# Seven block products for pairs of token blocks in the gate, and sums on GpSimd instead of VectorE, in a fp32 transformer layer

## The chip, the cores and the metric

The kernel runs on one core of one Trainium2 chip. The metric is the device time of one execution in microseconds (us), the median of several runs. The engines of a core are called by the profile's names: PE (TensorE, the matrix multiplier), DVE (VectorE), ACT (ScalarE), POOL (GpSimd) and SP (SyncE, which here issues most DMAs). Each engine works through its own list of instructions in order; an instruction that waits holds up all that stand behind it on its engine.

## What is computed

One layer of a transformer with 1024 tokens, a model width of 1024 and a feed-forward width of 4096, in fp32:

```
h = LN(alpha*x + concat(pool, attention) @ w_out)
h = LN(alpha*h + square(relu(h @ w_ff1)) @ w_ff2)
h = h + sigmoid(h @ w_ple_gate + b) * (p @ w_ple)
```

The change touches the end of the second line and the third line. There, `w_ple_gate` is 1024 x 1024, `p` is 1024 x 256 and `w_ple` is 256 x 1024.

## The kernel before

**Products.** Each fp32 product is made of three matmuls with shortened operands: an operand is split into a high part (a cast on ACT, `high`, line 98) and a low part (a subtraction of the high part from the operand, `low`, line 103, nearly always on the DVE). `mm3` (lines 112 to 115) then issues high x high, high x low and low x high. `add` (line 118) is any sum or difference of two tiles on the DVE. In the profile a group is named by its line, so all low parts made on the DVE have line 103 and are told apart by the tile that they write: `x` is the low part of a feed-forward weight (tile "x7"), `w` that of activations, `c` that of a gate weight, `ws` that of gate activations.

**Last feed-forward product.** The two feed-forward products are already made of block products of the kind that needs seven in place of eight, with sums of operands. The second one runs over units u = 0 to 55, seven products (their order is `SEQUENCE`, the last is product 2) by eight slices of the width 4096. A unit is 24 matmuls of 128x512. While TensorE works on unit u, `prepare(u + 1)` (line 781) makes the next operands: the sum of two activation blocks into a staging tile `st` of 128x1024 (line 118, two such tiles in turn), its high and low part, and the high and low part of the weight, which a DMA brought three units ahead. Units 48 to 55 are product 2. Beside them run: the second layer norm of token blocks 0 to 3 (`norm2`, `layer_norm`, lines 400 to 420), which lie in the tile `pre`; its last two steps are a scalar-tensor-tensor with the scale (line 419) and an add of the shift (line 420, shown as line 118), both on the whole 128x1024 block; the transposes of token blocks (`flip`, line 424, and a round trip through device memory); and the loads and splits of the gate's weights (`gate_load`, two more low parts `c` of 128x1024 for each call).

**Gate stage.** It goes through the token blocks n = 0 to 7 one after the other. Each block has two column halves of 512; a half takes 8 blocks of the inner dimension x 3 matmuls for the gate and 2 x 3 for `p @ w_ple`, so 60 matmuls of 128x512 for a token block (in the last block the second half is made in two pieces of 256 columns). `result` then adds the bias (line 929), takes the sigmoid on ACT (930), multiplies (931), adds the residual (932) and stores. The layer norm of blocks 4 to 7, the transposes and the splits of the next block run beside it.

**What sets the order.** The code is written as one stream; a scheduler with its own model of times places each engine's instructions, so the order on an engine is not that of the code. The layer norm's power (line 412) is POOL's only operation in this part of the program; POOL's earlier work consists of the pooling sums (line 361), a few splits, and DMA issues.

Of the kernel before, what the change touches and what calls it, by code (L numbers as in the profile page):

```python
# [7 lines left out]
F32 = mybir.dt.float32  # L8
F32R = mybir.dt.float32r
# [3 lines left out]
P = 128  # L13
# [46 lines left out]
}  # L60
BLOCK = {"a11": 0, "a12": 1, "a21": 2, "a22": 3}
NPRE = 8
NLAST = NPAIR - 4
AHEAD = 4

# [2 lines left out]
def layer(ctx, tc, xT, x, pT, w_in, w_pool, pscale, sinks, w_out, ln1, w1, w2, ln2, w_ple, w_gate, bgate, bias, rcount, out):  # L68
# [11 lines left out]
    def big(shape, dt=F32R):  # L80
        return sb.tile(shape, dt, tag="c", bufs=6, name=nm("c"))
# [14 lines left out]
    def high(dst, src, scale=None):  # L96
        if scale is None:
            nc.scalar.copy(out=dst, in_=src)  # L98
        else:
            nc.scalar.mul(out=dst, in_=src, mul=scale)  # L100

    def low(eng, dst, src, hi):
        return eng.tensor_tensor(out=dst, in0=src, in1=hi.bitcast(F32), op=ALU.subtract)  # L103

    def load_split(dst_h, dst_l, src, shape, eng, st=None, queue=None):
        st = stage(shape) if st is None else st
        load = (queue or nc.sync).dma_start(out=st, in_=src)
        high(dst_h, st)
        low(eng, dst_l, st, dst_h)
        return load  # L110

    def mm3(o, ah, al, bh, bl, first, last, more=False):
        nc.tensor.matmul(o, ah, bh, start=first, stop=False, skip_group_check=more)  # L113
        nc.tensor.matmul(o, ah, bl, start=False, stop=False, skip_group_check=more)  # L114
        nc.tensor.matmul(o, al, bh, start=False, stop=last, skip_group_check=more)  # L115

    def add(o, a, b, op=ALU.add):
        nc.vector.tensor_tensor(out=o, in0=a, in1=b, op=op)  # L118
# [278 lines left out]

    hn = [None] * NT

    def layer_norm(y, gb, root=False):  # L400
        st = small([P, 2, 6])
        for i in range(2):
            nc.vector.bn_stats(out=st[:, i, :], in_=y[:, i * HALF : (i + 1) * HALF])
        mv = small([P, 8])
        nc.vector.bn_aggr(out=mv[:, 0:2], in_=st.rearrange("p a b -> p (a b)"))
        v, r0, e, r, m = (mv[:, i : i + 1] for i in range(2, 7))
        nc.vector.tensor_scalar(out=v, in0=mv[:, 1:2], scalar1=LN_EPS, scalar2=None, op0=ALU.add)
        if root:
            nc.vector.reciprocal(out=r0, in_=v)
            nc.scalar.activation(out=r0, in_=r0, func=AF.Sqrt)  # L410
        else:
            nc.gpsimd.tensor_tensor(out=r0, in0=v, in1=mhalf, op=ALU.pow)
# [4 lines left out]
        nc.vector.tensor_scalar(out=m, in0=mv[:, 0:1], scalar1=-1.0, scalar2=None, op0=ALU.mult)  # L417
        nc.scalar.activation(out=y, in_=y, func=AF.Identity, bias=m, scale=1.0)
        nc.vector.scalar_tensor_tensor(out=y, in0=y, scalar=r, in1=gb[0], op0=ALU.mult, op1=ALU.mult)
# [98 lines left out]
    def temp(shape=(P, HALF)):  # L518
        return p1.tile(list(shape), F32, tag="t", bufs=6, name=nm("t"))
# [121 lines left out]
    def bank(shape=(P, HALF)):  # L641
        return pf.tile(list(shape), F32, tag="f", bufs=8, name=nm("f"))
# [81 lines left out]
    def incoming(shape=(P, 2, HALF)):  # L724
        return part(shape, F32)
# [44 lines left out]
    def hid(q, t, k):  # L770
        return hidden[q][:, k, t] if q in hidden else FF[q, k, t]
# [49 lines left out]
    def gate_load(j):  # L821
        if j == 0:
            gates["b"] = nat([P, D])
            nc.sync.dma_start(out=gates["b"], in_=bgate.partition_broadcast(P))
        w = gates[j] = big([P, 2, 2, D])
        src = w_gate[2 * j * P :] if j < 4 else (w_ple, pT)[j - 4]
        for k in range(2):
            load_split(w[:, 0, k], w[:, 1, k], src[k * P : (k + 1) * P, :], None, nc.vector, incoming((P, D)))

    flipped = {}  # L830

# [68 lines left out]


    b3, wl, pTs = gates["b"], gates[4], gates[5]
    for n in range(4, NT):
        norm2(n)
    for n in range(NT):
        if n + 1 < NT:
            h2s.append(gate_in(n + 1))
        if n + 2 < NT:
            gate_flip(n + 2)
        h2 = h2s[n]  # L910
        cols = [slice(0, HALF), slice(HALF, D)] if n < NT - 1 else [slice(0, HALF), slice(HALF, HALF + HALF // 2), slice(HALF + HALF // 2, D)]

        def ple(cs):
            o = bank()[:, 0 : cs.stop - cs.start]
            for k in range(2):
                pk = pTs[:, :, k, n * P : (n + 1) * P]
                mm3(o, pk[:, 0], pk[:, 1], wl[:, 0, k, cs], wl[:, 1, k, cs], k == 0, k == 1)
            return o

        def gate(cs):  # L920
            o = bank()[:, 0 : cs.stop - cs.start]
            for k in range(NK):
                w = gates[k // 2]
                mm3(o, h2[0][:, k, :], h2[1][:, k, :], w[:, 0, k % 2, cs], w[:, 1, k % 2, cs], k == 0, k == NK - 1)
            return o

        def result(cs, gt, pl):
            sg = temp()[:, 0 : cs.stop - cs.start]
            nc.vector.tensor_tensor(out=sg, in0=b3[:, cs], in1=gt, op=ALU.add)
            nc.scalar.activation(out=sg, in_=sg, func=AF.Sigmoid)  # L930
            nc.vector.tensor_tensor(out=sg, in0=sg, in1=pl, op=ALU.mult)
            nc.vector.tensor_tensor(out=sg, in0=sg, in1=acc[n][:, cs], op=ALU.add)
            nc.sync.dma_start(out=out[n * P : (n + 1) * P, cs], in_=sg)

        if n == 0:
            gts = [gate(cs) for cs in cols]
            for cs, gt in zip(cols, gts):
                result(cs, gt, ple(cs))
        else:
            for cs in cols:  # L940
                if cs.stop == D and n == NT - 1:
                    gt = gate(cs)
                    result(cs, gt, ple(cs))
                else:
                    pl = ple(cs)
                    result(cs, gate(cs), pl)
# [46 lines left out]
```

## Time and profile before

| | |
|---|---|
| median of 3 runs | 991.27 us (989.52 to 992.14) |
| the profiled execution | 990.92 us, of which the profile's span is 989.1 |
| gate stage in the span | from 875.64 to the last store |
| last feed-forward product (units 48 to 55) | 829.83 to 875.64 |

Two more lines of the page show where the data go. The first is the DMA share in 40 equal slices of the span, in tenths; the last five slices are the gate stage. The second gives what POOL does over the same slices.

```profile
POOL 0013552020010000100000000100011110001000
DMA  6512142622161543652363893675798776652411
```

POOL is nearly idle from the second quarter on; the DMA engines are busy for most of the feed-forward products and get quiet in the gate stage.

### The profile page before, as it was taken

The numbers are of one execution on the slowest core, as the hardware profiler recorded it, in microseconds if no ns is written. First come the engines' busy times: TensorE is split into PE (matmuls) and PEld (weight loads), VectorE is DVE, ScalarE is ACT, GpSimd is POOL, SyncE is SP. The second block draws the span as 40 slices with busy tenths as digits, with TensorE's granted clock in tenths as the row PEclk, the third lists the DMA queues.
The fourth block names the chain that finished last, engine by engine and source line by source line (L and its number), as shares of the span: only waits on it lengthen the run. The fifth ranks groups of instructions, "written<-read, shape, count | busy, mean of one in ns | idle before, by whom it ended". The sixth has DMA issues, their size and how long they took to land.

```text
span 989.1 us, 12163 instructions
## 1 busy us (share of the span) xinstructions
PE 980.2 (99%) x4498; PEld 814.0 (82%) x4498; DVE 718.7 (73%) x1137; ACT 457.6 (46%) x729; POOL 106.7 (11%) x142
## 2 busy tenths in 40 slices
PE   9999999999999999999999999999999999999998
PEld 7888887888888888888888888888888888778887
DVE  5798888895869777565446856887657699899533
ACT  5676666543576434444353433433434354553111
POOL 0013552020010000100000000100011110001000
PEclk9999999999999999999999999999999999999999
DMA  6512142622161543652363893675798776652411
GB/s 219 182 64 86 44 149 86 213 84 108 64 225 74 191 149 128 201 182 107 106 246 138 318 337 110 167 238 192 204 219 195 193 177 206 211 170 104 152 43 43
DMA packets 44763, 156.39 MB, mean 158 GB/s; under 512 B 5408, under 2 KB 10656, under 8 KB 41888
## 3 DMA queue, kind: packets, MB, share of 16 engines
q1 hardware_dynamic: 35280, 124.29, 36.6%
q0 software_dynamic: 7840, 26.74, 11.3%
q10 hardware_dynamic: 1584, 4.59, 1.2%
q8 instruction: 35, 0.57, 0.2%
q14 instruction: 24, 0.20, 0.1%
HBM read 128.86 MB, written 26.74 MB: 157 GB/s over the span
## 4 chain that ended last, share of the span: by engine, by line
PE 89%; DVE 5%; DMA 3%; issue 1%; ACT 1%; SPq 0%; DVEq 0%; ACTq 0%
PE f L114 20%; PE f L115 20%; PE f L113 20%; PE mm L113 8%; PE mm L115 8%; PE mm L114 8%; DMA ws<-in_w_gate 1%; DVE x L103 1%; PE pt L317 1%; DVE w L103 1%; PE s L294 1%; DMA ws<-in_w 1%; PE s L293 1%; DVE st L118 1%; PE av L323 1%
## 5 line engine op out<-in xcount | busy, mean ns | idle before, releaser
L114 PE MATMUL f<-x,w 128*128 128x512 f32 x448 | 174.8, 390 | 1.4 <-DVE x L103 1.2
L113 PE MATMUL f<-c,ws 128*128 128x512 f32 (+1 forms) x456 | 175.7, 385 | 0.0
L114 PE MATMUL f<-c,ws 128*128 128x512 f32 (+1 forms) x456 | 175.7, 385 | 0.0
L115 PE MATMUL f<-c,ws 128*128 128x512 f32 (+1 forms) x456 | 174.9, 386 | 0.0
L115 PE MATMUL f<-x,w 128*128 128x512 f32 x448 | 174.4, 389 | 0.0
L113 PE MATMUL f<-x,w 128*128 128x512 f32 x448 | 147.1, 389 | 0.0
L98 ACT CAST w<-st 128x1024 fp32r<-128x1024 f32 (+2 forms) x66 | 65.6, 998 | 104.0 <-issue 58.0
L103 DVE TENSOR_TENSOR w<-st,w 128x1024 fp32r<-128x1024 f32 (+2 forms) x66 | 77.4, 1176 | 44.6 <-ACT w L98 44.4
L114 PEld LDWEIGHTS f<-x,w 128*128 128x128 f32 x448 | 84.1, 188 | 20.7 <-DVE x L103 3.3
L115 PEld LDWEIGHTS f<-c,ws 128*128 128x128 f32 x456 | 85.7, 188 | 17.5 <-DVE ws L103 0.4
L114 PEld LDWEIGHTS f<-c,ws 128*128 128x128 f32 x456 | 85.7, 188 | 17.2
L113 PEld LDWEIGHTS f<-c,ws 128*128 128x128 f32 x456 | 85.7, 188 | 17.2
L113 PEld LDWEIGHTS f<-x,w 128*128 128x128 f32 x448 | 84.0, 188 | 17.6 <-ACT x L98 0.2
L115 PEld LDWEIGHTS f<-x,w 128*128 128x128 f32 x448 | 84.1, 188 | 17.3
L98 ACT CAST ws<-w 128x512 fp32r<-128x512 f32 x60 | 37.1, 622 | 57.8 <-PE f L115 42.4
L103 DVE TENSOR_TENSOR x<-ws,x 128x1024 fp32r<-128x1024 f32 x52 | 63.3, 1218 | 0.0
L118 DVE TENSOR_TENSOR n<-t,f 128x512 f32<-128x512 f32 x48 | 31.8, 684 | 39.3 <-PE f L115 39.2
L103 DVE TENSOR_TENSOR ws<-w,ws 128x512 fp32r<-128x512 f32 x60 | 41.1, 688 | 24.8 <-ACT ws L98 24.4
L98 ACT CAST ws<-st 128x512 fp32r<-128x512 f32 x48 | 29.8, 621 | 60.5 <-PE f L115 35.2
L113 PE MATMUL mm<-c,w 128*128 128x512 f32 x144 | 56.7, 399 | 0.2 <-ACT w L98 0.2
L115 PE MATMUL mm<-c,w 128*128 128x512 f32 x144 | 56.6, 394 | 0.0
L114 PE MATMUL mm<-c,w 128*128 128x512 f32 x144 | 56.5, 393 | 0.0
(210 smaller groups left out, 1811.9 us busy)
## 6 DMA issues: line engine op xcount, KB each, us to landing
ws<-in_w SPq DMA_DIRECT2D x70, 512.0 KB, 3.8
w<-in_w SPq DMA_DIRECT2D x16, 1024.0 KB, 5.0
c<-fd SPq DMA_DIRECT2D x6, 2048.0 KB, 8.6
fd<-n POOLq DMA_DIRECT2D x20, 512.0 KB, 3.5
ws<-in_w POOLq DMA_DIRECT2D x20, 512.0 KB, 7.9
st<-in_w_in SPq DMA_DIRECT2D x17, 512.0 KB, 3.3
w<-in_w SPq DMA_DIRECT2D x10, 512.0 KB, 4.1
n<-in_x SPq DMA_DIRECT2D x8, 512.0 KB, 5.7
```

The source lines that it names most:

```text
L98: nc.scalar.copy(out=dst, in_=src)
L103: return eng.tensor_tensor(out=dst, in0=src, in1=hi.bitcast(F32), op=ALU.subtract)
L113: nc.tensor.matmul(o, ah, bh, start=first, stop=False, skip_group_check=more)
L114: nc.tensor.matmul(o, ah, bl, start=False, stop=False, skip_group_check=more)
L115: nc.tensor.matmul(o, al, bh, start=False, stop=last, skip_group_check=more)
L118: nc.vector.tensor_tensor(out=o, in0=a, in1=b, op=op)
L293: nc.tensor.matmul(s[:, i, dst], ql, kt[:, 0, g, kk : kk + kn], start=True, stop=False)
L294: nc.tensor.matmul(s[:, i, dst], ql, kt[:, 1, g, kk : kk + kn], start=False, stop=True)
L317: nc.tensor.transpose(pt[:, i, :], e[:, i, kb * P : (kb + 1) * P], ident)
L323: nc.tensor.matmul(av, VV[0][:, blk, g], pp[:, 1], start=False, stop=(kb == 1))
```

## The change

The change has three parts.

1. *Gate.* Token blocks 0 to 3 are computed as before (`plain`). Blocks 4 to 7 are taken as two pairs, (4, 5) and (6, 7). In a pair the two token blocks are the two row halves, the inner dimension and the columns are halved too, and the eight products of half blocks become seven: W11, T2, T1, W21, T3, W22 and T4, where the T are sums of the weights' quarters. Each is 4 x 3 = 12 matmuls of 128x512, to which 24 of `p @ w_ple` come. In the last pair the products with T3 and T4, and part of the `p @ w_ple`, are made in pieces of 256 columns. The gate's weights are loaded as four quarters; the sums of quarters are made from rows that are read once more (`weight_sums` in blocks 1 and 2, `third_sums` and `fourth_sums` in the first pair), on the DVE, and split there and on ACT. `token_sums` makes three sums of transposed activations for a pair. Two adds of the bias in each pair (128x512) are on POOL.
2. *Second layer norm.* Its last add (128x1024) moves from the DVE to POOL for all eight token blocks.
3. *Activation sums.* Those of product 2 (eight of 128x1024, units 48 to 55) move from the DVE to POOL.

```diff
-    def layer_norm(y, gb, root=False):
+    def layer_norm(y, gb, root=False, eng=None):
...
-        add(y, y, gb[1])
+        (eng or nc.vector).tensor_tensor(out=y, in0=y, in1=gb[1], op=ALU.add)
...
-            add(sa, a, hid(q, *ta[1][:2]), SIGN[ta[1][2]])
+            (nc.gpsimd if i == 2 else nc.vector).tensor_tensor(out=sa, in0=a, in1=hid(q, *ta[1][:2]), op=SIGN[ta[1][2]])
...
-        w = gates[j] = big([P, 2, 2, D])
+        w = gates[j] = big([P, 2, 2, D] if j > 3 else [P, 2, 4, HALF])
...
     def norm2(n):
-        layer_norm(acc[n], gb2, n < 4)
+        layer_norm(acc[n], gb2, n < 4, nc.gpsimd)
...
+    def weight_sums(k):
+        if k == 0:
+            W["T1"] = wide("x7", [P, 2, 4, HALF], F32R)
+            W["T2"] = [wt([P, 2, 2, HALF]) for _ in range(2)]
+        if k % 2 == 0:
+            fourth.append(stage([P, 2, HALF]))
+        r = [incoming() for _ in range(2)]
+        for i in range(2):
+            nc.sync.dma_start(out=r[i], in_=w_gate[(4 * i + k) * P : (4 * i + k + 1) * P, :].rearrange("p (h c) -> p h c", h=2))
+        add(r[0][:, 0], r[0][:, 1], r[0][:, 0], ALU.subtract)
+        add(r[1][:, 1], r[1][:, 1], r[0][:, 0], ALU.subtract)
+        add(fourth[k // 2][:, k % 2], r[1][:, 0], r[1][:, 1], ALU.subtract)
+        split_k("T2", slice(k, k + 1), r[1][:, 1:2])
+        split_k("T1", slice(k, k + 1), r[0][:, 0:1])
+
+    def third_sums():
+        W["T3"] = big([P, 2, 4, HALF])
+        for k in range(4):
+            r = incoming()
+            for i in range(2):
+                nc.sync.dma_start(out=r[:, i : i + 1], in_=gate_rows(4 * i + k, 1, HALVES[1]))
+            add(r[:, 1], r[:, 1], r[:, 0], ALU.subtract)
+            split_k("T3", slice(k, k + 1), r[:, 1:2])
...
+    def token_sums(n):
+        f = [flipped.pop(n), flipped.pop(n + 1)]
+        s = part((P, 2, HALF), F32).rearrange("p s (R k c) -> p s R k c", R=4, k=4)
+        s1, s2, s3 = s[:, 0], s[:, 1], turned(f[1], 0)
+        add(s1, turned(f[1], 0), turned(f[1], 1))
+        add(s2, s1, turned(f[0], 0), ALU.subtract)
+        add(s3, turned(f[0], 0), turned(f[1], 0), ALU.subtract)
+        return f, s1, s2, s3
...
+    def pair(n):
...
+        gate_prod(A, a, "11")
+        nc.scalar.copy(out=u, in_=A)
+        c = tokens(s1)
+        Bk = bank()
+        gate_prod(Bk, b, "T2")
+        add(u, u, Bk)
+        nc.gpsimd.tensor_tensor(out=ur, in0=u, in1=b3[:, right_], op=ALU.add)
+        nc.gpsimd.tensor_tensor(out=u, in0=u, in1=b3[:, left], op=ALU.add)
...
+    for n in range(PLAIN):
...
+        plain(n)
+        if n in (1, 2):
             for k in range(2):
+                weight_sums(2 * n - 2 + k)
+    sums_of[PLAIN] = token_sums(PLAIN)
+    for n in range(PLAIN, NT, 2):
...
+        pair(n)
+        if n + 2 < NT:
+            sums_of[n + 2] = token_sums(n + 2)
```

Three places show how the instructions move. The first is the DVE in units 46 to 48, before the change. A row gives the line, the operation, the tile written and the tiles read; `st_6584` and `st_6617` are the activation sums of units 48 and 49, `x_703_4878<-ws_6417`, `ws_6467` and `ws_6501` the low parts of the weights of units 46, 47 and 48.

```order
L103 TENSOR_TENSOR x_703_4878<-ws_6417,x_703_4878 128x1024
L414 SCALAR_TENSOR_TENSOR sm_6688<-sm_6688 128x1
L118 TENSOR_TENSOR st_6584<-n_4580,n_4561 128x1024
L419 SCALAR_TENSOR_TENSOR pre_5033<-pre_5033,sm_6570,ws_6343 128x1024
L409 RECIPROCAL sm_6826<-sm_6826 128x1
L415 TENSOR_SCALAR sm_6688<-sm_6688 128x1
L424 STREAM_TRANSPOSE n_6847<-pre_5033 128x1024
L103 TENSOR_TENSOR w_6538<-st_6536,w_6538 128x1024
L118 TENSOR_TENSOR pre_5033<-pre_5033,ws_6344 128x1024
L416 TENSOR_TENSOR sm_6688<-sm_6688 128x1
L103 TENSOR_TENSOR x_703_4878<-ws_6467,x_703_4878 128x1024
```

The same engine there after the change (lines have moved down by two or more):

```order
L421 SCALAR_TENSOR_TENSOR pre_5033<-pre_5033,sm_6570,ws_6343 128x1024
L411 RECIPROCAL sm_6826<-sm_6826 128x1
L105 TENSOR_TENSOR x_703_4878<-ws_6417,x_703_4878 128x1024
...
L426 STREAM_TRANSPOSE n_6847<-pre_5033 128x1024
...
L105 TENSOR_TENSOR w_6538<-st_6536,w_6538 128x1024
...
L105 TENSOR_TENSOR x_703_4878<-ws_6467,x_703_4878 128x1024
L421 SCALAR_TENSOR_TENSOR pre_5033<-pre_5033,sm_6688,ws_6343 128x1024
L421 SCALAR_TENSOR_TENSOR pre_5033<-pre_5033,sm_6826,ws_6343 128x1024
L426 STREAM_TRANSPOSE n_6943<-pre_5033 128x1024
L105 TENSOR_TENSOR w_6586<-st_6584,w_6586 128x1024
L105 TENSOR_TENSOR x_703_4878<-ws_6501,x_703_4878 128x1024
```

The sums `st` and the adds into `pre` are gone from the DVE, the scalar-tensor-tensor for `sm_6570` stands ahead of unit 46's weight, and two more of them stand between the weights of units 47 and 48.

The second place is the end of POOL's list. Before the change the four powers of the last layer norms stand directly behind the last DMA issue:

```order
L740 DMA ws_6417<-in_w 128x1024
L740 DMA ws_6467<-in_w 128x1024
L412 TENSOR_TENSOR sm_6995<-sm_6995,mhalf 128x1
L412 TENSOR_TENSOR sm_7009<-sm_7009,mhalf 128x1
L412 TENSOR_TENSOR sm_7023<-sm_7023,mhalf 128x1
```

After it, twelve operations of 128x1024 stand between them, and four more follow among the powers (`n_5251` and the others are the token blocks 4 to 7):

```order
L742 DMA ws_6467<-in_w 128x1024
L422 TENSOR_TENSOR pre_5033<-pre_5033,ws_6344 128x1024
L789 TENSOR_TENSOR st_6584<-n_4580,n_4561 128x1024
L422 TENSOR_TENSOR pre_5033<-pre_5033,ws_6344 128x1024
L789 TENSOR_TENSOR st_6617<-n_4830,n_4795 128x1024
L422 TENSOR_TENSOR pre_5033<-pre_5033,ws_6344 128x1024 x2
L789 TENSOR_TENSOR st_6654<-c_4886 128x1024
...
L789 TENSOR_TENSOR st_6897<-c_5072 128x1024
L414 TENSOR_TENSOR sm_6995<-sm_6995,mhalf 128x1
...
L422 TENSOR_TENSOR n_5251<-n_5251,ws_6344 128x1024
```

So the powers of the last four layer norms now come behind all eight activation sums, and a norm add stands ahead of an activation sum in three places.

The third place is the DVE shortly before the first pair, after the change. `ws_7465` is the low part of the first pair's first activations; `x_968_7224` and `w_7226` are low parts of the weight sums T1 and T2, `st_7338` holds T4, `t` are results of blocks 1 to 3.

```order
L105 TENSOR_TENSOR x_968_7224<-ws_7339,x_968_7224 128x512
L120 TENSOR_TENSOR st_7338<-ws_7340 128x512
L120 TENSOR_TENSOR ws_7445<-n_7362 128x512
L105 TENSOR_TENSOR w_7226<-ws_7340,w_7226 128x512
L120 TENSOR_TENSOR ws_7350<-ws_7350 128x512
L120 TENSOR_TENSOR t_7401<-n_6737,f_7376 128x512
L120 TENSOR_TENSOR ws_7445<-ws_7445,n_7255 128x512
L120 TENSOR_TENSOR n_7362<-n_7255,n_7362 128x4x128
L120 TENSOR_TENSOR ws_7351<-ws_7351,ws_7350 128x512
L105 TENSOR_TENSOR ws_7465<-n_7255,ws_7465 128x4x4x32
```

Nothing of this stood there before but the result of a token block; all weight sums but the last and the three token sums stand ahead of the pair's first operand.

More of the change, by code (lines that the diff above doesn't have):

```diff
@@ L902, in layer, with ple, close @@
     b3, wl, pTs = gates["b"], gates[4], gates[5]
+    W = {"11": gates[0], "21": gates[1], "12": gates[2], "22": gates[3]}
+    def ple(n, cs):
+        o = bank()[:, 0 : cs.stop - cs.start]
+        for k in range(2):
+            pk = pTs[:, :, k, n * P : (n + 1) * P]
+            mm3(o, pk[:, 0], pk[:, 1], wl[:, 0, k, cs], wl[:, 1, k, cs], k == 0, k == 1)
+        return o
+    def close(n, cs, sg, pl):
+        nc.scalar.activation(out=sg, in_=sg, func=AF.Sigmoid)
+        nc.vector.tensor_tensor(out=sg, in0=sg, in1=pl, op=ALU.mult)
+        nc.vector.tensor_tensor(out=sg, in0=sg, in1=acc[n][:, cs], op=ALU.add)
+        nc.sync.dma_start(out=out[n * P : (n + 1) * P, cs], in_=sg)
@@ new lines, in gate, with plain, result @@
+    def gate(h2, i):
+        o = bank()
+        for k in range(NK):
+            w = W["12"[k // 4] + "12"[i]]
+            mm3(o, h2[0][:, k, :], h2[1][:, k, :], w[:, 0, k % 4], w[:, 1, k % 4], k == 0, k == NK - 1)
+        return o
+    def plain(n):
+        h2 = h2s[n]
+        def result(i, gt, pl):
+            sg = temp()
+            add(sg, b3[:, HALVES[i]], gt)
+            close(n, HALVES[i], sg, pl)
+        if n == 0:
+            gts = [gate(h2, i) for i in range(2)]
+            for i in range(2):
+                result(i, gts[i], ple(n, HALVES[i]))
+        else:
+            for i in (0, 1) if n < PLAIN - 1 else (1, 0):
+                pl = ple(n, HALVES[i])
+                result(i, gate(h2, i), pl)
@@ L903, in layer @@
+    sums_of = {}
     for n in range(4, NT):
         norm2(n)
-    for n in range(NT):
-        if n + 1 < NT:
+    for n in range(PLAIN):
+        if n + 1 < PLAIN:
             h2s.append(gate_in(n + 1))
@@ L909, in layer @@
             gate_flip(n + 2)
[L910 to L914, printed above, removed]
+        plain(n)
+        if n in (1, 2):
             for k in range(2):
[L916 to L946, printed above, removed]
+                weight_sums(2 * n - 2 + k)
+    sums_of[PLAIN] = token_sums(PLAIN)
+    for n in range(PLAIN, NT, 2):
+        if n + 2 < NT:
+            for i in range(2):
+                gate_flip(n + 2 + i)
+        pair(n)
+        if n + 2 < NT:
+            sums_of[n + 2] = token_sums(n + 2)
 _NAMES = ["xT", "x", "pT", "w_in", "w_pool", "pscale", "sinks", "w_out", "ln1", "w1", "w2", "ln2", "w_ple", "w_gate", "bgate", "bias", "rcount"]
```

79 lines of the change are left out of this document (76 added, 3 removed).

## The prediction

> **What bounds the kernel now.** I read the busy shares first, then the chain that ended last, then the windows, the list of waits and the timeline of the last quarter.
>
> ```profile
> PE 980.2 (99%) x4498; PEld 814.0 (82%) x4498; DVE 718.7 (73%) x1137; ACT 457.6 (46%) x729; POOL 106.7 (11%) x142
> PE 89%; DVE 5%; DMA 3%; issue 1%; ACT 1%; SPq 0%; DVEq 0%; ACTq 0%
> 300.00:400.00 100.00, 100.00 (x443) 82.81 (x442) 78.34 (x125) 46.79 (x78) 6.42 (x12) 1.00 0.37 134
> ```
>
> TensorE is busy for 99% of the span and carries 89% of the chain. The window from 300 to 400 us (columns: length, then busy time and count of PE, weight load, DVE, ACT, POOL, then granted clock, DMA share, GB/s) is a stretch with nothing but matmuls: 443 records in 100 us with a granted clock of 1.00, allowing for a few whose ends lie outside it 441, so one 128x512 matmul takes 100 / 441 = 0.2268 us of TensorE. A matmul less is time less, as long as its operands are there. Where are they late?
>
> ```profile
> 809.00:842.00 33.00, 32.78 (x145) 26.59 (x143) 33.00 (x47) 14.68 (x18) 0.60 (x1) 1.00 0.68 203
> 829.83:875.64 45.81, 44.49 (x193) 35.73 (x192) 41.49 (x41) 24.28 (x25) 0.00 (x0) 1.00 0.66 210
> 875.64:985.30 109.66, 109.66 (x511) 91.53 (x509) 69.79 (x113) 25.47 (x32) 4.22 (x4) 1.00 0.27 95
> PE f L114 <- DVE x L103: 1.2, 2, 0.8
> 842.57 0.50 PE L114 MATMUL f<-x,w 128*128 128x512 f32 x1 [0.79 <-DVE x L103]
> 870.98 0.50 PE L114 MATMUL f<-x,w 128*128 128x512 f32 x1 [0.42 <-DVE x L103]
> ```
>
> In the gate stage (875.64 to 985.30) TensorE never stops and the DVE is busy 69.79 of 109.66 us. Just ahead of it, in the last feed-forward product (units u48 to u55, 829.83 to 875.64), TensorE waits twice for the DVE's low part of a weight, at 842.57 and 870.98. That stage takes 45.81 us where its 8 x 24 matmuls need 192 x 0.2268 = 43.55: 2.26 us are lost. And from 809 to 842 the DVE is busy 33.00 of 33.00 us. This is the place to look at: the DVE sets the pace there, and POOL does nothing (0.60 us).
>
> **The change part by part.**
>
> *Fewer matmuls.* A pair of token blocks had 2 x 60 = 120 matmuls and gets 7 x 12 + 24 = 108. Two pairs save 24 of 128x512; the last pair's pieces of 256 columns number 60, as before. 24 x 0.2268 = **-5.44 us**. The chain after the last gate product (add, sigmoid, product, sum, store) keeps its form: nothing.
>
> *Sums that leave the DVE.* Eight activation sums and eight last adds of the second layer norm, all 128x1024, go to POOL.
>
> ```profile
> 816.72 1.22 DVE L103 TENSOR_TENSOR x<-ws,x 128x1024 fp32r<-128x1024 f32 x1
> 817.98 1.22 DVE L118 TENSOR_TENSOR st<-n,n 128x1024 f32<-128x1024 f32 x1
> 819.12 1.28 DVE L419 SCALAR_TENSOR_TENSOR pre<-pre,sm,ws 128x1024 f32<-128x1024 f32 x1
> 820.32 0.16 DVE L409 RECIPROCAL sm<-sm 128x1 f32<-128x1 f32 x1
> ...
> 828.70 1.22 DVE L103 TENSOR_TENSOR x<-ws,x 128x1024 fp32r<-128x1024 f32 x1
> 829.83 1.25 DVE L424 STREAM_TRANSPOSE n<-pre 128x1024 f32<-128x1024 f32 x1
> 829.83 1.07 PE L113 MATMUL f<-x,w 128*128 128x512 f32 x4
> 830.74 0.39 PE L114 MATMUL f<-x,w 128*128 128x512 f32 x1
> ```
>
> From start to start such a subtraction costs 828.70 to 829.83 = 1.13 us, the scalar-tensor-tensor 1.20 (819.12 to 820.32). If that were all, the 2.26 us lost in u48 to u55 would go as well: **-2.26 us**. But the operations now run beside the DVE, and the trace shows what the two engines do to each other:
>
> ```profile
> 83.81 1.06 POOL L361 TENSOR_TENSOR h<-h 128x527 f32<-128x527 f32 x1
> 120.97 1.17 POOL L361 TENSOR_TENSOR h<-h 128x527 f32<-128x527 f32 x1
> 121.70 1.53 DVE L103 TENSOR_TENSOR w<-st,w 128x1024 fp32r<-128x1024 f32 x1 [0.48 <-ACT w L98]
> 217.85 2.72 POOL L412 TENSOR_TENSOR sm<-sm,mhalf 128x1 f32<-128x1 f32 x1 [4.35 <-DVE sm L417]
> 217.75 1.22 DVE L103 TENSOR_TENSOR x<-n,x 128x1024 fp32r<-128x1024 f32 x1
> 218.88 1.28 DVE L103 TENSOR_TENSOR ws<-ws,ws 128x512 fp32r<-128x512 f32 x2
> ```
>
> At 121.70 a DVE subtraction starts while a POOL add runs (120.97 + 1.17 = 122.14); it ends at 123.23, which is 122.14 plus 1.09. It did nothing until POOL was done. At 217.85 the reverse: a POOL operation on one column lasts until the three DVE operations beside it have ended (220.16), then some 0.4. So a DVE operation with two SBUF inputs and a POOL operation take turns, whole instruction by whole instruction. The Trainium skill, page "SBUF — State Buffer", section "Who interferes with whom", states this rule: a DVE instruction with two SBUF inputs contends with a GpSimd instruction that reads SBUF, under an exclusive lock. The two rows above agree; by it the adds cost the DVE their own POOL duration, as in the sum below, and without it the result would be that of the first rival.
>
> *What a POOL add of 128x1024 costs.* No row has one. The nearest:
>
> ```profile
> 41.82 1.30 POOL L103 TENSOR_TENSOR wp<-st,wp 128x512 fp32r<-128x512 f32 x1 [25.52 <-ACT wp L98]
> 104.83 1.06 POOL L361 TENSOR_TENSOR h<-h 128x525 f32<-128x525 f32 x1
> 105.98 1.05 POOL L361 TENSOR_TENSOR h<-h 128x521 f32<-128x521 f32 x1
> 89.36 1.29 POOL L361 TENSOR_TENSOR h<-h 128x513 f32<-128x513 f32 x1
> L369 POOL TENSOR_TENSOR h<-h,rc 128x1 f32<-128x1 f32 x1 | 0.2, 191 | 1.5 <-DVE h L364 1.5
> ```
>
> One column costs 0.19 and 512 columns 1.06 to 1.30. By the code of line 361 the adds of 527, 525 and 521 columns (1.06) read two inputs that start 1, 2 and 4 elements apart; the one of 513 columns (1.29) has them 8 apart, and the subtraction of whole tiles takes 1.30. The moved adds read whole tiles, so I take the latter price: 2 x 1.30 - 0.19 = **2.41 us**; the ends are 2 x 1.06 - 0.19 = 1.93 and 2 x 1.30 = 2.60. The Trainium skill, page "GPSIMD Engine Reference", its table of measured `tensor_tensor` adds, gives 4497 ns for 2048 columns, 1.96 times the DVE, and from that the rule to keep elementwise work on the DVE; half of that is an estimate of 2.25, by which the sum below would come out about 1 us lower. No row here shows it.
>
> *u46 to u48, laid end to end.* Here x is the low part of a unit's weight (line 103, `x<-ws,x`), w that of its activations. In the changed program the DVE's long rows are: scalar-tensor-tensor, x (u46), transpose, w, x (u47), two scalar-tensor-tensors, transpose, w, x (u48); POOL's are: sum of u48, add, sum of u49, add, add. u46's x started at 816.72. The scalar-tensor-tensor that stood behind it (819.12) now stands ahead of it, and POOL's sum of u48, free to start, gets in: x starts at 816.72 + 1.20 + 2.41 = 820.33. From there: x 1.13, POOL 2.41, w 1.13, POOL 2.41, x 1.13, twice 1.20, POOL 2.41 (the transpose beside it), w 1.13, POOL 2.41, x 1.13 = 17.69, which ends at 838.0. TensorE wants u48's x after its first four matmuls, at 830.74. **+7.2 us**, five POOL operations of 2.41 in place of three DVE ones of 1.13. At 1.93 each it is +4.8; if three of the five hide beside transposes and other work that does not contend, about 0. Behind u48 a unit needs w, x and one POOL sum, 2 x 1.13 + 2.41 = 4.67 us of a unit's 24 x 0.2268 = 5.44, so the later waits go; units with two gate subtractions (c) more need 6.93. Four of those are 6.0 us too much. Against that stands 45.81 - 41.49 = 4.32 us in which the DVE idled there before, and some 1.6 in hand: u50's x ends at 838.0 + 2 x 4.67 = 847.3, wanted at 830.74 + 10.88 + 7.2 = 848.8. Between 0 and 4.3 (none of the idle time usable) I take **+1.0**.
>
> *Gate stage, DVE up to the first pair.*
>
> ```profile
> L103 DVE TENSOR_TENSOR ws<-n,ws 128x1024 fp32r<-128x1024 f32 x6 | 7.3, 1212 | 0.0
> L118 DVE TENSOR_TENSOR n<-n,ws 128x1024 f32<-128x1024 f32 x4 | 4.8, 1196 | 0.0
> L929 DVE TENSOR_TENSOR t<-n,f 128x512 f32<-128x512 f32 x7 | 4.7, 676 | 1.5 <-PE f L115 1.5
> L931 DVE TENSOR_TENSOR t<-t,f 128x512 f32<-128x512 f32 x7 | 4.6, 667 | 0.1
> 870.84 1.28 DVE L118 TENSOR_TENSOR n<-n,f 128x512 f32<-128x512 f32 x2
> 872.03 3.49 DVE L103 TENSOR_TENSOR c<-ws,c 128x1024 fp32r<-128x1024 f32 x3
> 930.38 0.39 PE L113 MATMUL f<-c,c 128*128 128x512 f32 x1
> ```
>
> The groups (busy, mean ns, idle before) are cut to 875.64 to 930.10, four blocks of TensorE work; the DVE idles 1.6 us in it (1.5 before L929, 0.1 before L931). Out go four adds (4 x 1.13) and two of six lows (2 x 1.13), 6.8. In come, ahead of the first pair's operand, 11 weight adds and 6 lows of 128x512 at (872.03 - 870.84) / 2 = 0.60 (10.2), three token sums (1.8), half a low (0.6): 12.6. 5.8 more than before, 4.2 more than it has room for; and four POOL adds of 2.41 that can block it, 9.6, about half of them beside PSUM adds and transposes. Against that stand the units' sums that no longer hold it. Between 0 and 5.2 I take **+3.0**: TensorE then waits, shortly after 930.38, for the low part of the first pair's first activations. POOL's four adds of 128x512 in the pairs have TensorE products of 12 x 0.2268 = 2.72 us to hide under: nothing. ACT (25.47 of 109.66) and the queues (DMA share 0.27) have room for the re-read weights: nothing, up to 1 if the third weight sum comes late.
>
> *Sum* against the profiled run's own 990.92 (span 989.1 and 1.82 around it): -5.44 - 2.26 + 7.2 + 1.0 + 3.0 = +3.5, so 994.4; the median of the three runs lies 0.35 higher, which gives 994.8. I say **994.6 us**.
>
> **The rivals.**
>
> - *POOL's adds slip beside the DVE* (faster). In its favour: transposes, PSUM adds and bn_stats run from 809 on, the DVE's stream is full and POOL did get its turn behind three operations at 217.85, so it may only fill gaps. Against: 33.00 of 33.00 us busy, and u48's w itself waits for a POOL sum. Then -5.44 - 2.26 + 1 = -6.7: 984.
> - *The adds block, but at the low price* (no change): 1.93 us each, as the misaligned rows: -5.44 - 2.26 + 4.8 + 0 + 2.0 = -0.9: 990. It decides between this and the forecast what one 128x1024 add on POOL measures; break-even lies near 2.1.
> - *POOL wins every gap* (slower still): it enters after each DVE instruction, once more ahead of u46 (+2.41) and in the gate stage (+2): 999.
>
> **How the numbers follow.** Forecast 0.45, of which most is slower by over 0.3% (3.0 us, about what a measurement of this kernel can tell from no change), 0.35, and 0.10 within; POOL slips beside 0.26, nearly all faster; low price 0.21, within but for 0.03 faster; POOL wins 0.08. Faster 0.28, same 0.28, slower 0.44. Since cases of both signs hold most of the chance, the forecast's own range is 991.5 to 998; the range for 8 in 10 leaves out the lower part of the first rival and the upper end of the last: 984 to 999.
>
> **What would show it.** Right: PE waits on DVE x of some 1.5 to 4 us between 819 and 838, none at u50 and u55; POOL adds of 128x1024 near 2.4 us; DVE subtractions stretched to 3 us beside them; a wait of 2 to 4 us near 931 to 940 at the first pair; 24 matmuls fewer. Wrong: adds near 1.9 us, or stretched POOL rows beside DVE rows at their old 1.22 (POOL yields, not the DVE); no waits before 876, which means the sums fitted.

## The result, and the profile after

| | before | changed |
|---|---|---|
| median | 990.83 us (4 runs, 989.52 to 992.14) | 1002.37 us (4 runs, 1000.12 to 1004.43) |
| ratio to before, 95% interval | | 1.0116 (1.0089 to 1.0142) |
| profiled execution, span | 989.1 us | 1002.7 us |

The changed kernel is 11.5 us slower; the profiled execution, at 1004.43 the slowest of the four, shows 13.6 us more in its span. Where are they? First the same lines of the page as before: busy time of the engines and the chain.

```profile
PE 980.9 (98%) x4474; PEld 811.7 (81%) x4474; DVE 759.6 (76%) x1174; ACT 472.3 (47%) x755; POOL 161.6 (16%) x162
PE 83%; DVE 10%; DMA 3%; issue 2%; POOL 1%; ACT 0%; SPq 0%; DVEq 0%; ACTq 0%
```

TensorE has 24 matmuls fewer in its list and 24 records fewer in the trace, and yet it is busy as long as before (980.9 against 980.2): some of its matmuls have become longer. The DVE holds twice as much of the chain. The list of TensorE's waits (who waits, for whom; then us in total, number of waits, the longest), first for the feed-forward units (800 to 890 us, first row), then for the gate stage (890 to 1003 us), and under it the three waits of the gate stage one by one:

```profile
PE f L116 <- DVE x L105: 8.5, 5, 5.4
PE f L115 <- ACT ws L100: 3.7, 2, 2.7
PE f L117 <- DVE ws L105: 1.7, 1, 1.7
929.41 0.50 PE L115 MATMUL f<-c,ws 128*128 128x512 f32 x1 [1.08 <-ACT ws L100]
944.75 0.80 PE L115 MATMUL f<-c,ws 128*128 128x512 f32 x1 [2.66 <-ACT ws L100]
947.66 0.80 PE L117 MATMUL f<-c,ws 128*128 128x512 f32 x1 [1.69 <-DVE ws L105]
```

Five waits for the low part of a weight (`x`), 8.5 us together, where before there were two with 1.2 us; and in the gate stage, which had none, 5.4 us for activations: 1.08 at the start of token block 3, then 2.66 and 1.69 at the first product of the first pair. The next lines are the windows of the changed kernel, with the same columns as before (the last but two is the granted clock, the share of its full clock that TensorE was given): first the stretch that the prediction looked at, then the longest wait, the matmuls behind it, a stretch after those, and the matmuls behind the wait of 2.66 us in the gate stage.

```profile
809.00:842.00 33.00, 24.71 (x101) 19.16 (x100) 33.00 (x33) 11.77 (x14) 23.37 (x8) 0.95 0.50 149
834.00:839.80 5.80, 0.43 (x2) 0.00 (x1) 5.80 (x4) 1.61 (x2) 5.80 (x3) 0.90 0.34 128
839.83:845.51 5.68, 5.68 (x13) 4.45 (x14) 4.39 (x3) 0.00 (x0) 4.52 (x2) 0.50 0.84 250
845.51:851.50 5.99, 5.99 (x28) 4.94 (x27) 2.36 (x2) 2.00 (x2) 2.68 (x2) 1.00 0.60 203
944.75:951.24 6.49, 4.80 (x10) 3.31 (x11) 6.49 (x12) 3.89 (x7) 0.00 (x0) 0.50 0.14 34
```

From 809 to 842 the DVE is as full as before, POOL is busy for 23.37 us instead of 0.60, and TensorE does 101 matmuls instead of 145. The third row explains the longer matmuls: behind the long wait TensorE runs at a granted clock of 0.50, 13 matmuls in 5.68 us where 13 x 0.2268 = 2.95 would do, so 2.7 us more. In the last row it is 6.49 - 1.69 (a second wait) - 10 x 0.2268 = 2.5 us.

The account of the span: 24 matmuls less, -5.4; the waits of before gone, -1.2; waits in the units +8.5; slow matmuls behind them +2.7; waits in the gate stage +5.4; slow matmuls there +2.5. Together +12.5 of 13.6 us. The rest fits the restart after each of the eight waits. At the first one the row names 1.19 us, while from the start of the four matmuls ahead of it to the next, 815.52 - 813.26 = 2.26 us, 2.26 - 4 x 0.2268 = 1.35 us are too much:

```profile
813.26 1.07 PE L115 MATMUL f<-x,w 128*128 128x512 f32 x4
815.52 0.50 PE L116 MATMUL f<-x,w 128*128 128x512 f32 x1 [1.19 <-DVE x L105]
```

How POOL and the DVE meet in the longest wait shows in the timeline (start, duration, engine, line; the wait is TensorE's 834.4 to 839.83):

```profile
832.05 6.64 POOL L422 TENSOR_TENSOR pre<-pre,ws 128x1024 f32<-128x1024 f32 x2 [1.16 <-DVE pre L421]
838.66 3.35 POOL L789 TENSOR_TENSOR st<-c 128x1024 f32<-128x1024 f32 x1
833.09 1.23 DVE L426 STREAM_TRANSPOSE n<-pre 128x1024 f32<-128x1024 f32 x1
834.25 2.24 DVE L105 TENSOR_TENSOR w<-st,w 128x1024 fp32r<-128x1024 f32 x1
836.42 3.36 DVE L105 TENSOR_TENSOR x<-ws,x 128x1024 fp32r<-128x1024 f32 x1
839.83 0.79 PE L116 MATMUL f<-x,w 128*128 128x512 f32 x1 [5.41 <-DVE x L105]
909.10 2.40 POOL L422 TENSOR_TENSOR n<-n,ws 128x1024 f32<-128x1024 f32 x1 [1.12 <-DVE sm L409]
909.13 2.39 DVE L416 SCALAR_TENSOR_TENSOR sm<-sm 128x1 f32<-128x1 f32 x1
```

Unhindered, a POOL add of 128x1024 takes 2.40 us (909.10); beside the DVE it takes 3.3 (6.64 for two), because it waits 1 us for the DVE's turn first. The DVE's subtraction, 1.22 us long when alone (1.13 from start to start), becomes 2.24 and 3.36. One after the other, in strict turns: add, w, add, x, sum. The transpose at 833.09, which reads one tile, keeps its 1.23 us beside POOL's add, so of the operations here it is those with two SBUF inputs that are held. Even such an operation on one column, which the DVE does in 0.2 us, sat out POOL's whole add (909.13, 2.39 us).

### The profile page after: what moved, and what is told of

It reads as the page before. It is cut to its first block, busy times and chain, and to the rows that moved or that the text cites. A ratio compares the mean times of both kernels' runs of the same rounds, so it can differ in the third digit from the quotient of the medians.

```text
span 1002.7 us, 12239 instructions
## 1 busy us (share of the span) xinstructions
PE 980.9 (98%) x4474; PEld 811.7 (81%) x4474; DVE 759.6 (76%) x1174; ACT 472.3 (47%) x755; POOL 161.6 (16%) x162
## 4 chain that ended last, share of the span: by engine, by line
PE 83%; DVE 10%; DMA 3%; issue 2%; POOL 1%; ACT 0%; SPq 0%; DVEq 0%; ACTq 0%
PE f L117 18%; PE f L116 18%; PE f L115 18%; PE mm L116 8%; PE mm L117 8%; PE mm L115 7%; DMA ws<-in_w_gate 2%; DVE x L105 2%; DVE c L105 1%; DVE w L105 1%; PE pt L319 1%; PE s L296 1%; PE s L295 1%; DVE sm L405 1%; DMA n<-in_xT 1%
## 5 line engine op out<-in xcount | busy, mean ns | idle before, releaser
L115 PE MATMUL f<-c,ws 128*128 128x512 f32 (+1 forms) x420 | 163.8, 390 | 3.7 <-ACT ws L100 3.7
L117 PE MATMUL f<-c,ws 128*128 128x512 f32 (+1 forms) x420 | 162.8, 390 | 1.7 <-DVE ws L105 1.7
L116 PE MATMUL f<-c,ws 128*128 128x512 f32 (+1 forms) x420 | 163.3, 389 | 0.0
L105 DVE TENSOR_TENSOR w<-st,w 128x1024 fp32r<-128x1024 f32 (+2 forms) x66 | 82.1, 1245 | 52.8 <-ACT w L100 52.7
L115 PEld LDWEIGHTS f<-c,ws 128*128 128x128 f32 x420 | 79.4, 189 | 20.5 <-ACT ws L100 4.6
L117 PEld LDWEIGHTS f<-c,ws 128*128 128x128 f32 x420 | 79.3, 189 | 19.6 <-DVE ws L105 3.4
L116 PEld LDWEIGHTS f<-c,ws 128*128 128x128 f32 x420 | 79.4, 189 | 16.2
L105 DVE TENSOR_TENSOR x<-ws,x 128x1024 fp32r<-128x1024 f32 (+1 forms) x56 | 70.3, 1255 | 0.0
L100 ACT CAST x<-ws 128x1024 fp32r<-128x1024 f32 (+1 forms) x56 | 56.9, 1017 | 13.8 <-DVE ws L120 13.8
L115 PE MATMUL mm<-c,w 128*128 128x512 f32 x144 | 56.4, 396 | 0.1
L116 PE MATMUL mm<-c,w 128*128 128x512 f32 x144 | 56.3, 392 | 0.1
```

## The experiments

Two theories stood against each other. **A**: POOL's adds and the DVE's operations with two SBUF inputs take turns, and this costs the time. **B**: the pairs themselves cost it, with their second reading of the weights and their sums. The changes of the kernels are small, so only their lines are shown.

**The parts one by one.** Pairs only:

```diff
-            (nc.gpsimd if i == 2 else nc.vector).tensor_tensor(out=sa, in0=a, in1=hid(q, *ta[1][:2]), op=SIGN[ta[1][2]])
+            add(sa, a, hid(q, *ta[1][:2]), SIGN[ta[1][2]])
...
-        layer_norm(acc[n], gb2, n < 4, nc.gpsimd)
+        layer_norm(acc[n], gb2, n < 4)
```

> The pairs of the gate alone; all sums and all norm adds stay on the DVE. Theory A (POOL's adds and the DVE's subtractions take turns, and that is what costs): the waits of units 45 to 49 go back to those of before (1.2 us in all, no granted clock of 0.5 there), the 24 matmuls are saved (-5.4), and the gate stage keeps a wait of 0 to 5 us, since the DVE then has four more adds of 1.13 us ahead of the first pair: 986 to 992 us. Theory B (the pairs themselves cost: the weights read a second time and their sums come late): the gate stage loses 6 us or more in waits and 2 us at half clock as in the changed kernel, so 993 to 997 us.

The kernel before with these two moves to POOL, without the pairs:

> The gate as before (no pairs); the eight activation sums and the eight norm adds on POOL. Theory A: waits of about 8.5 us for the low part of a weight in units 45 to 49 and some 2.7 us at half clock behind the longest, nothing in the gate stage (its DVE was busy 70 of 110 us), the waits of before gone (-2): 999 to 1001 us. Theory B: the loss lies in the gate stage, so this kernel lies within 3 us of before, 988 to 994 us.

Pairs with the first of the two lines above undone, so that only the norm adds are on POOL, and pairs with the second undone, so that only the sums are there:

> Pairs and norm adds on POOL; the activation sums stay on the DVE. Theory A: four POOL adds of 2.4 us among the DVE's work of units 45 to 49 in place of four of 1.13 us: waits there of 2 to 5 us, gate stage with waits of 3 to 6 us: 991 to 999 us. If the waits of units 45 to 49 come from the sums alone, they are gone here: 990 to 993 us.

> Pairs and activation sums on POOL; the norm adds stay on the DVE. Theory A: POOL's sums of units 48 to 50 take turns with the DVE, waits of 3 to 6 us in units 46 to 50, then none; the gate stage loses 2 to 6 us: 990 to 998 us. If the norm adds alone cause the long wait at unit 48 (two of them stand ahead of it), no wait above 1.5 us is left in the units, and 988 to 992 us come out.

| kernel | median us | ratio to before (interval) | waits in units | waits in gate stage |
|---|---|---|---|---|
| pairs only | 992.84 | 1.0026 (1.0014 to 1.0038) | 1.0 | 5.6 |
| both moves, no pairs | 999.07 | 1.0090 (1.0074 to 1.0105) | 7.6 | 0 |
| pairs, norm adds on POOL | 1004.01 | 1.0135 (1.0119 to 1.0150) | 5.9 | 6.9 |
| pairs, sums on POOL | 996.62 | 1.0063 (1.0050 to 1.0076) | 4.6 | 3.6 |
| changed kernel | 1002.37 | 1.0116 (1.0089 to 1.0142) | 8.5 | 5.4 |

The waits, in us, are those of the lists of waits of the profiled executions. The rows of the first two kernels, from 780 us on (both moves, then pairs only in two rows):

```profile
PE f L114 <- DVE x L103: 7.6, 4, 5.4
PE f L115 <- ACT ws L100: 5.6, 3, 4.0
PE f L116 <- DVE x L105: 1.0, 2, 0.8
```

Both theories hold a part; the pairs alone lie between the two ranges that had been expected. The moves to POOL cost 8.5 us alone, all of it in the units (A). But the pairs alone lose their 5.4 us and 2.2 more, by waits in the gate stage in which POOL has no add of this size (B). Neither move alone is harmless: the norm adds on POOL beside the pairs cost 11.2 us, the sums 3.8. The sums alone came out as expected; the norm adds alone lie above the 991 to 999 us that were expected for them. Their median is even 1.6 us above that of both moves together, but the two intervals overlap, so that this difference is not shown.

**Is it the shared path, or where the sums stand?** The kernel before once more, every row of the DVE in its old order, and POOL doing additional work that nobody waits for:

```diff
             add(sa, a, hid(q, *ta[1][:2]), SIGN[ta[1][2]])
+            if i == 2:
+                for j in range(4):
+                    piece = sa[:, j // 2, j % 2 * 256 : j % 2 * 256 + 256]
+                    nc.gpsimd.tensor_tensor(out=unused, in0=piece, in1=piece, op=ALU.add)
```

> The kernel before, with its DVE order unchanged; in units 48 to 55 POOL adds each activation sum to itself into a tile that nobody reads (four adds of 128x256 for a unit, 32 in all). Theory A, that POOL's adds and the DVE's two-input operations take turns: each of POOL's adds (some 0.6 us by the 2.40 us of 1024 columns) holds the DVE up, some 2.4 us for a unit where the DVE had less than 0.5 us to spare in units 46 to 50: waits of 4 to 10 us for the low part of a weight, 996 to 1005 us. Rival: the changed kernel's waits came from where the sums and adds stand and from their longer duration, not from the shared path: the DVE's rows keep their 1.22 us and the time is that of before within 1.5 us.

996.01 us, ratio 1.0059 (1.0045 to 1.0073): at the low end of what A expected, far outside the rival. The timeline of this kernel, DVE and POOL at unit 49, its list of waits in the units and the gate stage, and the longest of these waits with the window behind it:

```profile
832.20 1.63 DVE L118 TENSOR_TENSOR st<-c 128x1024 f32<-128x1024 f32 x1
833.82 1.21 DVE L103 TENSOR_TENSOR w<-st,w 128x1024 fp32r<-128x1024 f32 x1
834.96 1.63 DVE L103 TENSOR_TENSOR x<-ws,x 128x1024 fp32r<-128x1024 f32 x1
836.51 1.63 DVE L419 SCALAR_TENSOR_TENSOR pre<-pre,sm,ws 128x1024 f32<-128x1024 f32 x1
833.97 5.34 POOL L792 TENSOR_TENSOR unused<-st 128x256 f32<-128x256 f32 x4 [1.23 <-DVE sm L416]
PE f L114 <- DVE x L103: 4.7, 4, 2.3
844.70 0.50 PE L114 MATMUL f<-x,w 128*128 128x512 f32 x1 [2.32 <-DVE x L103]
844.50:848.00 3.50, 3.30 (x9) 2.65 (x10) 3.50 (x4) 0.00 (x0) 3.34 (x3) 0.64 0.73 234
```

Many DVE rows are stretched from 1.22 to 1.63 us, and POOL's four small adds take 5.34 us. No result of POOL was needed anywhere. Another way in which POOL could hold the DVE is the staging tile, which the DVE may not overwrite while POOL still reads it; but the DVE's own list of waits from 800 to 880 us has no row. So the cost comes from the two engines excluding each other: 5.8 us, with the slow matmuls behind the wait of 2.32. What the rest of the 8.5 us of both moves comes from, POOL's longer sums or the new order, is not separated. One short add stretches a DVE operation by 0.41 us (1.63 in place of 1.22), where one long add stretched it by 1 to 2 us.

**What holds the pairs back.** Two kernels with the pairs, all sums and norm adds on the DVE, and without the weight sums T1, T2 and T4 (quarters of the weights take their place, so that the result is not that of the layer); the second still reads the weights a second time:

```diff
     def weight_sums(k):
...
+        W["T1"], W["T2"] = W["11"], W["21"]
...
     def fourth_sums():
...
+        W["T4"] = W["22"]
```

> The pairs alone (sums and norm adds on the DVE), but the weight sums T1, T2 and T4 are left out, with their second reading of the weights; the products take quarters of the weights in their place. DVE as the bound of the gate stage: 10 to 12 us of DVE work less, the waits of 6.1 us and the 2.0 us at half clock at the first pair go, and 984 to 987 us come out. If the waits come from the chain of transposes and round trips of blocks 4 and 5, more than 3 us of waits stay, 989 us or more.

> As the kernel without weight sums, but with the second reading of the weights (eight transfers of 512 KB) left in and unused. If the DVE's work was the bound, the time is that of the kernel without sums within 1 us. If the transfers are (the DMA engines were 80 to 98% busy from 905 to 930 in the pairs alone, and the transposes' round trips go through the same queue), waits of 3 us or more stay at the first pair and it is 2 us or more slower than the kernel without sums.

Without the sums 986.45 us (0.9961; 0.9948 to 0.9975), with the unused reads 984.46 (0.9941; 0.9928 to 0.9954). In neither did TensorE wait in the gate stage; the lists from 780 us on have one row each, for waits in the units:

```profile
PE f L116 <- DVE x L105: 1.5, 3, 0.8
PE f L116 <- DVE x L105: 0.8, 1, 0.8
```

So the traffic of the reads costs nothing, and the sums on the DVE (twelve differences and eight low parts of 128x512 at 0.60 us, 12 us) are what holds the pairs back; with them away, 4.1 and 6.1 us of gain show, where 24 matmuls are 5.4. (The second kernel was expected within 1 us of the first. The 2 us between them, the one with more transfers being the faster, stay unexplained; the waits in the units account for 0.7.) The window of the pairs alone from the gate's start to the end of its waits at the first pair says the same: the DVE is busy 58.62 of 60.60 us. ACT, which has fewer high parts to make without the sums, is busy for only 22.48 us of it. The 2.0 us in which the DVE is idle are three waits for the rows that are read once more (last row); what they are worth, unused reads can't show, but it is less than the 5.6 us that TensorE waits.

```profile
874.40:935.00 60.60, 55.59 (x243) 45.08 (x241) 58.62 (x102) 22.48 (x29) 4.21 (x4) 0.97 0.55 182
DVE ws L120 <- DMA ws<-in_w_gate: 2.0, 3, 1.5
```

**Can the pair come later, or its first products be others?** One pair only, all sums and norm adds on the DVE:

```diff
-PLAIN = 4
+PLAIN = 6
```

> All sums and norm adds on the DVE, and only blocks 6 and 7 as a pair (blocks 0 to 5 as before). If the gate stage loses because the DVE has 12 us of weight and token sums too many before the first pair, this pair begins 27 us later, where the DVE of before was idle for more than half of the time (9.91 of 25 us busy from 925): no wait over 0.5 us, 12 matmuls of 0.2268 us saved, 2.7 us faster than before, 987 to 989 us. If it loses because of something that the pairs bring themselves (their chain of products and sums, reads of the weights), waits of 1 to 4 us come with this pair as well, and it is 990 to 993 us.

988.31 us, ratio 0.9978 (0.9967 to 0.9988): 2.3 us faster than before, of 2.7 expected. This is the one version found that computes the layer and beats both kernels. TensorE's list of waits from 780 us on has one row, the old wait at unit 50, and the windows show that the DVE has room there:

```profile
PE f L116 <- DVE x L105: 0.8, 1, 0.8
900.00:925.00 25.00, 25.00 (x112) 20.68 (x111) 23.71 (x35) 6.36 (x10) 0.00 (x0) 1.00 0.79 261
925.00:950.00 25.00, 25.00 (x112) 20.62 (x111) 20.12 (x30) 8.68 (x12) 0.00 (x0) 1.00 0.44 149
```

The other way was to keep both pairs and begin each with W11 and W21, which need no sums, with the weight sums in their place or one token block later:

```diff
         a = tokens(turned(f[0], 0))
+        d = tokens(turned(f[0], 1))
...
         gate_prod(A, a, "11")
         nc.scalar.copy(out=u, in_=A)
+        p11 = ple(n, left)
+        gate_prod(A, d, "21", True)
...
+        b = tokens(s2)
```

> As the kernel with the two products first, but with the weight sums where the changed kernel has them. The low part of the first pair's first activations still stands behind nearly all weight sums on the DVE: the wait of 1.2 us at the first product stays or grows to 3, the one of 4.0 us at T2 goes: 986 to 990 us, slower than with the later sums if the place of the sums counts.

> Both pairs, all sums and norm adds on the DVE; in a pair the two products that need no sums (W11, W21) come first, with the first product of p and w_ple between them, so that T2 is due 18 matmuls (4.1 us) later, and the weight sums are made one token block later. If the DVE's backlog of about 5 us at the first pair is all that held the pairs back, the waits there fall from 6.1 us to below 2, no half clock follows, and it is 985.5 to 988 us, faster than before and than one pair alone. If the DVE's work up to the pair is simply too much wherever it stands, waits of 4 us or more stay, and it is 989 us or more.

993.53 us (1.0031; 1.0019 to 1.0044) and 995.94 (1.0065; 1.0045 to 1.0086). The expectation for the first, 986 to 990 us, failed. The longest wait shrank from 4.0 to 2.2 us, and no slow matmuls followed, but the sum of the waits in the gate stage stayed (6.3 us against 5.6): TensorE then waits for the next operand. For the second, two outcomes had been named, and the one for a DVE with too much to do wherever its work stands came true (989 us or more, waits of 4 or more: 7.4 in its gate stage). A later place for the sums did not help; the median is 2.4 us higher. Up to the first pairs the DVE has too much to do, in both orders that were tried.

**The half clock.** Does a wait alone bring it, without any work on POOL? The kernel before, with extra DVE operations that change no value, in a table from unit to number:

```diff
+EXTRA = {11: 4, 18: 6, 25: 7, 32: 8, 39: 10}
...
+        for _ in range(EXTRA.get(u, 0)):
+            nc.vector.tensor_tensor(out=b[0], in0=b[0], in1=b[0], op=ALU.max)
```

> The kernel before, with 4, 6, 7, 8 and 10 extra DVE operations of 128x1024 (1.13 us each, which change no value) ahead of one weight's split in units 11, 18, 25, 32 and 39 of the second feed-forward product, so that TensorE waits there for 1 to 7 us. If a long wait itself brings the half clock, the longer ones are followed by matmuls at 0.427 us for some 5 us, and the shorter ones (below some 2.5 us) by none, and the time is the sum of the waits plus 0.2 us for each slow matmul. If the half clock came with what POOL does, no wait here brings it.

1021.11 us (2 runs). The rows are four of the timeline's waits, and the windows behind each of them in the same order:

```profile
740.13 0.80 PE L115 MATMUL f<-x,w 128*128 128x512 f32 x1 [4.49 <-DVE x L104]
779.47 0.50 PE L115 MATMUL f<-x,w 128*128 128x512 f32 x1 [3.60 <-DVE x L104]
804.34 2.14 PE L114 MATMUL f<-x,w 128*128 128x512 f32 x8 [2.12 <-ACT x L99]
817.46 1.82 PE L114 MATMUL f<-x,w 128*128 128x512 f32 x4 [1.91 <-ACT x L99]
740.00:746.00 6.00, 5.87 (x14) 4.62 (x15) 5.93 (x7) 0.00 (x0) 0.86 (x1) 0.50 0.45 102
779.50:783.00 3.50, 3.50 (x10) 2.77 (x11) 3.50 (x4) 0.00 (x0) 0.00 (x0) 0.61 0.41 150
806.00:812.00 6.00, 6.00 (x29) 4.95 (x28) 2.01 (x2) 0.00 (x0) 0.11 (x1) 1.00 0.55 175
817.00:821.00 4.00, 3.54 (x9) 2.69 (x10) 4.00 (x5) 2.30 (x3) 0.00 (x0) 0.60 0.26 73
```

Behind 4.49 and 3.60 us the granted clock falls to 0.50 and 0.61, behind 2.12 it stays at 1.00, and behind 3.60 us POOL is idle. So it is the wait. The edge is not sharp. A wait of 2.24 us brought no fall (in the pairs that begin with W11 and W21 and have the sums in their old place; first row and window below), one of 2.32 did (0.64, in the kernel with the idle adds, shown there). But against the expectation the wait of 1.91 us, 13 us behind the one of 2.12, was followed by 0.60. And two waits close together can do it: 1.46 us, with some 1.2 us of matmuls between it and a wait of 0.86, was followed by 0.50 (in this kernel; last row and window).

```profile
935.38 0.50 PE L115 MATMUL f<-w,ws 128*128 128x512 f32 x1 [2.24 <-ACT ws L100]
931.00:940.00 9.00, 6.15 (x24) 4.37 (x25) 9.00 (x17) 3.48 (x6) 0.00 (x0) 1.00 0.33 99
906.65 0.80 PE L116 MATMUL f<-c,ws 128*128 128x512 f32 x1 [1.46 <-DVE ws L104]
906.60:909.50 2.90, 2.85 (x7) 2.28 (x8) 2.90 (x5) 1.05 (x1) 0.00 (x0) 0.50 0.13 52
```

The Trainium skill, page "TensorE: Matmul & The Clock Gate", Part 1, says that an idle window of some 3.4 us brings TensorE to half rate and that some 3.4 us of activity bring it back. The return agrees in order (5.7 us at half clock behind the longest wait of the changed kernel); the fall does not: 2.32 us were enough, and the measurement decides.

**The price of a POOL add.** The prediction took 2.41 us because the inputs of the moved adds start at the same place within a row. This kernel is the changed one with the shift of the norm stored one column off:

```diff
+            eng.tensor_tensor(out=y[:, 0:1], in0=y[:, 0:1], in1=gb[1][:, D - 1 :], op=ALU.add)
+            eng.tensor_tensor(out=y[:, 1:], in0=y[:, 1:], in1=gb[1][:, 0 : D - 1], op=ALU.add)
```

> The changed kernel, with the shift of the layer norm stored one column off, so that POOL's norm add reads two inputs that start one element apart (and one column apart for itself). If the start of the inputs sets the price, as the rows of 1.06 and 1.29 us in the trace of before suggest, the unhindered norm adds take 1.9 to 2.0 us instead of 2.40, and the time falls by 2 to 5 us from 1002.4. If it was something else, they take 2.4 us and 0.2 more for the column, and the time is 1002 to 1005 us.

The adds of 1023 columns took the same:

```profile
906.52 2.41 POOL L426 TENSOR_TENSOR n<-n,ws 128x1023 f32<-128x1023 f32 x1
910.53 2.39 POOL L426 TENSOR_TENSOR n<-n,ws 128x1023 f32<-128x1023 f32 x1
```

The start of the inputs does not set the price; why the 527-column adds of before took 1.06 us and not 1.3 stays open. The time, 1000.20 us (1.0100; 1.0085 to 1.0115), lies below the 1002 to 1005 expected for this price; its interval overlaps with that of the changed kernel.

## Why the prediction was off

Its sign was right, and so was the turn-taking of POOL and the DVE; its size was not: +3.5 us in the sum, 11.5 measured (13.6 in the profiled execution), and 1002.4 lies above the range's upper end of 999.

- **24 matmuls, -5.44 us.** Right: 24 are gone, and where nothing held them up (the kernel without sums and with unused reads) the gain was 6.1 us by the medians of that comparison (990.59 and 984.46); without the reads it was 4.1.
- **The waits of before go, -2.26.** Nearly right; those at units 50 and 55 became one of 0.2 us. Behind the slow matmuls the last 175 of the stage took 40.23 us (845.51 to 885.74), 0.5 more than 175 x 0.2268.
- **u46 to u48 laid end to end, +7.2, and +1.0 behind it.** Right in size for the three units: 1.38, 0.31 and 5.41 us, 7.1 together. The prediction spread them over some of 1.5 to 4 us; the one of 5.41 came about since two norm adds stood in turn with the w and x of unit 48. That the whole sum of 8.2 is so near the 8.5 measured is partly luck: the wait of 1.19 us at unit 45, behind a norm add, was not foreseen, and in place of the 1.0 behind unit 48 came 0.2.
- **POOL add 2.41.** The number was right (2.40), its reason, the start of the inputs, was not (the run with the shifted column), so that the choice between 2.41 and 1.93 came out right by luck.
- **Nothing for the clock.** This is the first step that failed, and the larger one: the sum counted a wait at its own length, and nothing for what stands behind it. A wait of 5.41 us and one of 2.66 brought the granted clock to 0.50 for 13 and 10 matmuls, 2.7 + 2.5 = 5.2 us that no term held. The run with extra DVE operations shows that the wait is the cause. Some 1.1 us more lie in the restarts after the waits, which had no term either.
- **Gate stage, +3.0, "between 0 and 5.2".** This is the second step that failed: 5.4 us of waits. The prediction's own terms were 4.2 us over the DVE's room and about half of the 9.6 us of POOL's four adds, some 9 us; it then let the units' lighter DVE pay for most of that, and its upper end of 5.2 does not follow from these terms. How much of them was paid in this way is open: the waits are longer than the forecast and shorter than the terms. What the runs show is that the weight sums on the DVE are needed for the waits (none without them), and that moving the four norm adds to POOL gives no relief: in the profiled executions the gate stage waits 6.9 and 5.4 us with them on POOL, 5.6 and 3.6 with them on the DVE.
- **The rivals.** "POOL's adds slip beside the DVE" fell with the idle adds, which nobody waited for, and the low price with the adds of 2.40 us. "POOL wins every gap" came nearest in time (999), and the trace shows not a winner but strict turns.

## What to carry to other kernels

Moving work from a full DVE to an idle POOL did not relieve the DVE here, because its operations beside it read two SBUF inputs: count each POOL add at its whole duration on the DVE's own time line, not at nothing. (Beside transposes it would not have to be counted, by the row at 833.09; no run here moved work to such a place.) A saving on TensorE that is paid with sums on another engine is worth what that engine has free *before* the first product that needs them; the second half of the saving, put behind a stretch in which the DVE had time for the sums, was the half that came out. And a TensorE wait of some 2.3 us or more cost slow matmuls on top in these runs (2.7 us behind 5.41, 2.5 behind 2.66 and 1.69), so one long wait is worse than several short ones of the same sum that stand apart (1.40, 2.24, 0.58 and 2.08 us in the pairs begun with W11 and W21 cost none).

## What the runs showed of the hardware that was not expected

- The two engines alternate one instruction each: two POOL adds in 6.64 us with a DVE subtraction stretched to 3.36 between them, rather than one engine keeping the path.
- A DVE operation of one column with two inputs was held for 2.39 us by a POOL add (909.13 of the changed kernel).
- Half clock followed a wait of 2.32 us but not one of 2.24; it also followed one of 1.91 us, 13 us behind another, and one of 1.46 us, 1.2 us behind another; it lasted 13 matmuls behind 5.41 us and 10 behind 2.66 and 1.69.
- A transpose, which reads one tile, kept its 1.23 us while a POOL add ran beside it (833.09 of the changed kernel).
